# A two-layer attention trunk on one core: layer 0's elementwise work on SBUF goes to POOL, its last gate runs by contraction tiles, the last pair's weights come in six transfers

## The chip, the core and the metric

One core of a Trainium2 chip runs the whole program. Its engines are TensorE (PE, matrix products; loading the weights of one is shown apart, as PEld), VectorE (DVE), ScalarE (ACT), GpSimd (POOL) and SyncE (SP), which here issues all transfers, in order, on one queue. Each engine works through its own instructions in a fixed order and waits at semaphores for the others. PE writes to PSUM; DVE and ACT read PSUM and SBUF; POOL works on SBUF alone here. The metric is the device time of one execution in microseconds.

## What is computed

Two decoder layers over 1024 tokens of width 1024, float32. Each is `h + rmsnorm(mixer(rmsnorm(h)))`. The change is in layer 0, whose mixer is attention in three groups (g = 0, 1, 2) of 16 heads, with dilations 1, 4 and 16; the groups are combined by their softmax denominators, gated and projected:

```
for g, (window, dil) in enumerate(DIL_GROUPS):
    o, lse = dilated_window_attention(q[:, :, sl], k[:, :, sl], v[:, :, sl], window, dil)
alpha = jax.nn.softmax(jnp.stack(lses, axis=0), axis=0)
o = jnp.sum(alpha[..., None] * jnp.stack(outs, axis=0), axis=0)
y = o.reshape(B, S, DIL_WIDTH).astype(h.dtype) * jax.nn.silu(gate)
return y @ w_out
```

Layer 1 is causal differential attention with 8 heads, a norm per head and the same kind of gate.

## The kernel before

**Split operands.** A product needs more precision than one pass gives, so each operand is kept as a high part, rounded to the matmul's type by a copy on ACT, and a low part, the difference, made by `low` (line 122). A projection tile is then three matmuls of 128x512: high by high, low by high, high by low (`project`, line 271). `split` (line 183) makes the two parts of a weight tile, `wh` and `wl`; without a named engine its subtraction alternates between DVE and POOL (`alt`, line 126). The normed input lies in SBUF as XH and XL, by eight contraction tiles kt.

**Order.** PE's order is that of the program text. The order on the other engines is set by a scheduler at build time, from estimates. Tiles come from pools with few buffers, and an instruction that needs a buffer again waits for its last reader.

**Layer 0 up to 400 us** makes the values, seven of the eight gates and their stores. **From 400 us on** it runs a loop over 48 heads (8 pairs of heads, 3 groups, 2 heads), four steps each. A step scores two blocks (`scores`, line 582; DVE adds the mask and takes the maximum, line 603, ACT the exponential), three steps later transposes the probabilities (`transposes`, 611; PE writes `tp`, ACT copies the high part, DVE makes the low part `pp`, line 122), and two steps after that multiplies by the values (`product`, 627). Between these, a filler hands PE the matmuls of the query and key projections to come, one unit per pair and group (`qk_unit`, 220): PE fills two PSUM banks, DVE multiplies them by cos and sin into the tiles t (lines 247 to 251, three buffers), POOL adds and subtracts them into r (250, 252), ACT rounds r to rh (256), and `low` subtracts (DVE and POOL in turn). A unit's parts go to DRAM and come back as the head's qh, ql and ka (`heads_in`, 261).

Group 2 has one block of keys per query block, so its product (`alone`, 654) ends in eight additions per pair: DVE adds the two passes out of PSUM into `us_` (666), ACT copies the upper half to `ul` (667, one buffer), DVE adds both into the group's output tile u (669). Groups 0 and 1 end in `store` (671), whose addition (679) reads PSUM.

**Combination.** When a pair's last scores are done, the statistics go to DRAM (`put_stats`) and come back as js; `joint` (701) forms the weights in eleven small DVE instructions and stores them as wt_d. `combine` (726) loads them spread over 64 partitions as wb (a transfer of 64x512 for each half of the tokens, group and head: 12 a pair, three buffers), multiplies the three u tiles by them (735, DVE and POOL in turn; DVE alone for pair 7), adds them (740), multiplies by the gate sil_in (741) and hands the result to `put_y` (368), which splits it and stores it as y_d. The u tiles have three buffers, so that pair p+1's first u tile is pair p's y.

**End of layer 0.** After the last unit the filler makes the last gate (`late_gates`, `gate_units`, 278): contraction tiles 0 to 3 for both token halves, then 4 to 7. Then `out_early` (420) loads y of the first pairs into XH and XL (`load_y`, 395, each tile as soon as the gate is done with it), multiplies it by the output weights into partial sums, which ACT copies (444) and SP stores in XH and XL (447), and waits for the last heads. `out_rest` closes with the later tiles. Layer 1 has the same tail.

## Time and profile before

| | us |
|---|---|
| median of 3 runs (2026.72 to 2030.63) | 2029.63 |
| the profiled execution | 2031.38 |
| its span in the trace | 2029.5 |
| PE busy in the span | 1905.9 |
| DVE, ACT, POOL busy | 1143.0, 888.0, 618.0 |

The span runs from the first to the last instruction in the trace; the execution is 1.9 us longer. Busy shares are means over stages that differ: layer 0's heads run from 400 to about 1290 us, layer 1's from about 1440 to 1950 us. Matmuls overlap in the trace (a 128x512 one lasts 0.40 us and starts 0.23 us after the one before), so a window in which PE is busy throughout can't be much shortened.

### The profile page before, as it was taken

The numbers are of one execution on the slowest core, as the hardware profiler recorded it, in microseconds if no ns is written. First come the engines' busy times: TensorE is split into PE (matmuls) and PEld (weight loads), VectorE is DVE, ScalarE is ACT, GpSimd is POOL, SyncE is SP. The second block draws the span as 40 slices with busy tenths as digits, with TensorE's granted clock in tenths as the row PEclk, the third lists the DMA queues.
The fourth block names the chain that finished last, engine by engine and source line by source line (L and its number), as shares of the span: only waits on it lengthen the run. The fifth ranks groups of instructions, "written<-read, shape, count | busy, mean of one in ns | idle before, by whom it ended". The sixth has DMA issues, their size and how long they took to land.

```text
span 2029.5 us, 28888 instructions
## 1 busy us (share of the span) xinstructions
PE 1905.9 (94%) x10008; PEld 1594.5 (79%) x10008; DVE 1143.0 (56%) x2771; ACT 888.0 (44%) x2057; POOL 618.0 (30%) x386
## 2 busy tenths in 40 slices
PE   6999999999999998989898978899999999999898
PEld 4788888888878787878787867788878788887776
DVE  3312122146676768676768674571057877878626
ACT  3312122125555555555555565352244445545632
POOL 2000000043353535353535340040471533524111
PEclk8999999999999999999999989999999999999999
DMA  5424244377696969697878889553356555555753
GB/s 208 146 88 140 87 156 152 113 221 229 191 300 195 291 202 293 195 282 218 267 234 240 256 284 294 162 176 107 129 174 193 175 176 164 169 196 182 274 160 125
DMA packets 218018, 397.90 MB, mean 196 GB/s; under 512 B 40976, under 2 KB 123408, under 8 KB 217872
## 3 DMA queue, kind: packets, MB, share of 16 engines
q1 hardware_dynamic: 217872, 396.04, 61.3%
q8 instruction: 80, 1.31, 0.3%
q14 instruction: 66, 0.54, 0.1%
HBM read 254.87 MB, written 132.71 MB: 191 GB/s over the span
## 4 chain that ended last, share of the span: by engine, by line
PE 62%; DMA 13%; DVE 12%; ACT 4%; POOL 4%; issue 3%; SPq 1%; POOLq 0%; DVEq 0%; ACTq 0%
PE pqk L274 22%; PE pv L213 16%; PE pg L274 8%; PE po L386 4%; PE sc L921 2%; PE pe L439 2%; PE up L646 2%; PE sc L596 2%; DMA wb<-wt_d 2%; PE ob L974 2%; DMA st_d<-st 2%; PE tp L619 2%; DVE u L669 1%; POOL r L252 1%; DVE pm L924 1%
## 5 line engine op out<-in xcount | busy, mean ns | idle before, releaser
L274 PE MATMUL pqk<-XL,wh 128*128 128x512 f32 x1024 | 421.1, 411 | 0.0
L274 PE MATMUL pqk<-XH,wh 128*128 128x512 f32 x1024 | 409.3, 400 | 1.7 <-DVE t L251 1.7
L274 PE MATMUL pqk<-XH,wl 128*128 128x512 f32 x1024 | 410.5, 401 | 0.0
L606 ACT ACTIVATE pm<-pm,st 128x128 f32<-128x128 f32 (+1 forms) x384 | 170.2, 444 | 159.7 <-DVE st L603 158.1
L122 POOL TENSOR_TENSOR wl<-raw,wh 128x1024 fp32r<-128x1024 f32 x35 | 84.0, 2400 | 500.6 <-ACT wh L184 500.6
L274 PEld LDWEIGHTS pqk<-XH,wh 128*128 128x128 f32 x1024 | 194.3, 190 | 30.6 <-DVE t L251 2.4
L274 PEld LDWEIGHTS pqk<-XL,wh 128*128 128x128 f32 x1024 | 194.4, 190 | 27.5
L274 PEld LDWEIGHTS pqk<-XH,wl 128*128 128x128 f32 x1024 | 194.8, 190 | 27.0
L250 POOL TENSOR_TENSOR r<-t 128x512 f32<-128x512 f32 x64 | 98.2, 1535 | 266.7 <-DVE t L249 265.7
L122 DVE TENSOR_TENSOR wl<-raw,wh 128x1024 fp32r<-128x1024 f32 x61 | 82.0, 1345 | 149.1 <-ACT wh L184 148.6
L213 PE MATMUL pv<-vwh,XH 128*128 128x512 f32 x384 | 155.8, 406 | 7.0 <-ACT XH L158 4.0
L184 ACT CAST wh<-raw 128x1024 fp32r<-128x1024 f32 x96 | 100.5, 1047 | 140.3 <-PE pqk L274 61.8
L213 PE MATMUL pv<-vwl,XH 128*128 128x512 f32 x384 | 154.9, 403 | 2.8 <-POOL vwl L122 2.8
L213 PE MATMUL pv<-vwh,XL 128*128 128x512 f32 x384 | 154.8, 403 | 0.9 <-DVE XL L122 0.3
L122 DVE TENSOR_TENSOR vs<-pv,vs 128x512 fp32r<-128x512 f32 x64 | 44.2, 691 | 197.3 <-ACT vs L513 191.3
L931 ACT ACTIVATE pm<-pm,mx 128x256 f32<-128x256 f32 (+7 forms) x128 | 99.4, 776 | 120.3 <-DVE mx L930 61.8
L122 DVE TENSOR_TENSOR pp<-tp,pp 128x512 fp32r<-128x512 f32 (+2 forms) x192 | 104.0, 542 | 73.6 <-ACT pp L623 72.0
L619 PE MATMUL tp<-ident,pm 128*128 128x128 f32 x560 | 95.7, 279 | 39.2 <-DVE pp L122 38.2
L603 DVE CUSTOM_DVE_ANT_0 pm<-sc,masks 128x128 f32<-128x128 f32 (+1 forms) x384 | 118.8, 344 | 20.8 <-PE sc L596 19.4
L619 PEld LDWEIGHTS tp<-ident,pm 128*128 128x128 f32 x560 | 72.6, 143 | 73.5 <-issue 34.2
L924 DVE CUSTOM_DVE_ANT_0 pm<-sc,md 128x512 f32<-128x512 f32 (+3 forms) x192 | 102.5, 551 | 32.9 <-PE sc L921 30.1
L513 ACT CAST vs<-pv 128x512 fp32r<-128x512 f32 x48 | 28.2, 587 | 189.9 <-PE pv L213 188.7
(514 smaller groups left out, 4483.6 us busy)
## 6 DMA issues: line engine op xcount, KB each, us to landing
qk_d<-rh SPq DMA_DIRECT2D x64, 512.0 KB
qk_d<-r SPq DMA_DIRECT2D x64, 512.0 KB
qh<-qk_d SPq DMA_DIRECT2D x128, 256.0 KB
ql<-qk_d SPq DMA_DIRECT2D x128, 256.0 KB
ka<-qk_d SPq DMA_DIRECT2D x64, 512.0 KB
v_d<-vs SPq DMA_DIRECT2D x48, 512.0 KB
raw<-in_dil_qk_dram SPq DMA_DIRECT2D x48, 512.0 KB
vt<-v_d SPq DMA_DIRECT2D x48, 512.0 KB
```

The costliest lines, as they stand in the source:

```text
L122: eng.tensor_tensor(o, full, hi.bitcast(F32), ALU.subtract)
L184: nc.scalar.copy(wh, raw)
L213: nc.tensor.matmul(o, lhsT=l, rhs=r_, start=first and k == 0, stop=last and k == 3 * KT - 1, skip_group_check=True)
L250: nc.gpsimd.tensor_sub(put(r[0]), nat(t1), nat(t2))
L274: nc.tensor.matmul(o, lhsT=l[:, kt, :], rhs=r_[:, kt, tok], start=kt == 0 and k == 0, stop=kt == KT - 1 and k == 2)
L386: nc.tensor.matmul(banks[c], lhsT=l[:, kt, ts(n)], rhs=r_[:, ts(c, 512)], start=first and k == 0, stop=last and k == 2,)
L439: nc.tensor.matmul(bank, lhsT=l[:, kt, ts(n)], rhs=r_[:, ts(c, 512)], start=kt == 0 and k == 0, stop=kt == EARLY - 1 and k == 2)
L603: nc.vector.tensor_tensor_reduce(pm[:, cols], sc[:, cols], m[:, m.shape[1] - w_ :], 1.0, 3.0e38, ALU.add, ALU.min, st[:, 0, j : j + 1])
L606: nc.scalar.activation(pm[:, cols], pm[:, cols], AF.Exp, bias=st[:, 0, j : j + 1], scale=-1.0, accum_out=st[:, 1, j : j + 1])
L619: nc.tensor.transpose(out=tp[:, ts(n)], in_=self.pb.pop((b, kb)), identity=ident)
L924: nc.vector.tensor_tensor_reduce(pm[:, k0:k1], sc[:, :w_], m_, 1.0, 3.0e38, ALU.add, ALU.min, mx[:, j : j + 1])
L931: nc.scalar.activation(pm[:, :wq], pm[:, :wq], AF.Exp, bias=mx[:, 0:1], scale=-1.0, accum_out=den)
```

## The change

- `qk_unit`: in layer 0 POOL makes all `wl` and all low parts of r; layer 1 stays as it was.
- `alone`: the last addition (669, now 672) goes from DVE to POOL.
- `combine`: for pairs 0 to 6 POOL does all of it, the two halves of `put_y` included (the rounding copy was ACT's, the difference DVE's). It goes in the order of groups 0, 2, 1, adding as it goes, and the result is built in group 2's tile. The gate tile uses the wb buffers, and u has four buffers. For pair 7 DVE does it as before, with the weights of a head and group in one transfer of 64x1024: six in place of twelve.
- `gate_units`: the last gate of either layer takes tiles 0 and 1 for both halves, then one tile at a time.
- Smaller pools (sr, js, jm, je with one buffer) make room.

```diff
@@ qk_unit
-            split(wh, wl, load(w[half], [P, KT, P]))
+            split(wh, wl, load(w[half], [P, KT, P]), None if on_pool else nc.gpsimd)
...
-            low(nc.vector if on_pool else alt(), r[e].bitcast(F32R), r[e], rh)
+            low(nc.vector if on_pool else nc.gpsimd, r[e].bitcast(F32R), r[e], rh)
@@ gate_units
-                for k0 in (0, EARLY):
+                for kts in ((0, 1), *((kt,) for kt in range(2, KT))):
                     for c in range(2):
-                        yield from project(banks[c], wh, wl, ts(c, 512), range(k0, k0 + EARLY))
+                        yield from project(banks[c], wh, wl, ts(c, 512), kts)
@@ put_y(layer, kt, c, y, hi, eng=None)
-        nc.scalar.copy(hi, y)
-        low(nc.vector, y.bitcast(F32R), y, hi)
+        if eng is None:
+            nc.scalar.copy(hi, y)
+        else:
+            eng.tensor_copy(hi, y)
+        low(eng or nc.vector, y.bitcast(F32R), y, hi)
@@ alone
-                nc.vector.tensor_add(by_residue(uo, SUB[2])[:, 2 * c : 2 * c + 2, :], us_[:HD], ul)
+                nc.gpsimd.tensor_add(by_residue(uo, SUB[2])[:, 2 * c : 2 * c + 2, :], us_[:HD], ul)
@@ combine
+            eng = nc.vector if pr == 7 else nc.gpsimd
+            full = {}
+            if pr == 7:
+                for g, tag in ((0, "v"), (2, "v"), (1, "pp")):
+                    full[g] = lp.tile([P, T], F32R, tag=tag, name="wb").bitcast(F32)
+                    for h in range(2):
+                        nc.sync.dma_start(full[g][64 * h : 64 * h + 64], wt_d[2 * pr + h, g].partition_broadcast(64))
             for c in range(2):
                 tok = ts(c, 512)
-                for g in range(NG):
-                    wb = lp.tile([P, 512], F32, tag="wb", name="wb", bufs=3)
...
-                    (nc.vector if pr == 7 else alt()).tensor_mul(us[g][:, tok], us[g][:, tok], wb)
-                sil = lp.tile([P, 512], F32, tag="sil_in", name="sil_in", bufs=1)
+                y = us[2][:, tok]
+                for g in (0, 2, 1):
+                    if full:
+                        wb = full[g][:, tok]
+                    else:
+                        wb = lp.tile([P, 512], F32, tag="wb", name="wb", bufs=3)
...
+                    eng.tensor_mul(us[g][:, tok], us[g][:, tok], wb)
+                    if g:
+                        eng.tensor_add(y, y, us[1 if g == 1 else 0][:, tok])
+                sil = lp.tile([P, 512], F32, tag="wb", name="sil_in", bufs=3)
                 nc.sync.dma_start(sil, sil_d[0][pr, :, tok])
-                y = us[0][:, tok]
-                for g in (1, 2):
-                    (nc.vector if pr == 7 else nc.gpsimd).tensor_add(y, y, us[g][:, tok])
-                nc.vector.tensor_mul(y, y, sil)
-                put_y(0, pr, c, y, us[1][:, tok])
+                eng.tensor_mul(y, y, sil)
+                put_y(0, pr, c, y, us[1][:, tok], eng)
@@ the loop over heads
-                    us[hd.pr, hd.g] = lp.tile([P, T], F32, tag="u", name="u", bufs=3)
+                    us[hd.pr, hd.g] = lp.tile([P, T], F32, tag="u", name="u", bufs=4)
```

In the whole program DVE issues 24 `wl`, 24 low parts of r, 64 additions of `alone`, 21 weight multiplications, 14 gate multiplications and 14 low parts of y fewer, ACT 14 copies fewer, and POOL these and no others more; PE issues the same matmuls in the same number. The lines of the changed kernel are shifted (603 is 606, 666 is 669, 669 is 672, 679 is 682, 735 is 750, 740 is 752, 741 is 755).

Where the order of the engines changes, in three places. First DVE in pair 0's combination, from the sixth addition of `alone` on. Before:

```order
L666 TENSOR_TENSOR us__3776<-us__3776,up_3773 128x256
L669 TENSOR_TENSOR u_3270<-us__3776,ul_3777 64x2x128
L735 TENSOR_TENSOR u_2602<-u_2602,wb_3900 128x512
L122 TENSOR_TENSOR pp_3806<-tp_3801,pp_3806 128x512
L666 TENSOR_TENSOR us__3816<-us__3816,up_3813 128x256
L603 ISA pm_3827,st_3652<-sc_3826,masks_2246 128x128
L603 ISA st_3652 128x1
L603 ISA pm_3827,st_3652<-sc_3826,masks_2246 128x256
L603 ISA st_3652 128x1
L669 TENSOR_TENSOR u_3270<-us__3816,ul_3817 64x2x128
L249 TENSOR_TENSOR t_3863<-pqk_3783,sin_2236 128x512
L122 TENSOR_TENSOR wl_4293<-raw_4294,wh_4292 128x1024
```

and now:

```order
L669 TENSOR_TENSOR us__3776<-us__3776,up_3773 128x256
L122 TENSOR_TENSOR pp_3806<-tp_3801,pp_3806 128x512
L669 TENSOR_TENSOR us__3816<-us__3816,up_3813 128x256
L606 ISA pm_3827,st_3652<-sc_3826,masks_2246 128x128
L606 ISA st_3652 128x1
L606 ISA pm_3827,st_3652<-sc_3826,masks_2246 128x256
L606 ISA st_3652 128x1
L249 TENSOR_TENSOR t_3863<-pqk_3783,sin_2236 128x512
```

Gone from between the low parts `pp` and the maxima are the weight multiplication, both additions into u and the `wl`; a little further down so are two more multiplications and a low part of r.

Second, POOL in the same place, from the `wl` before the first weight multiplication to the first r of the next unit. Before:

```order
L122 TENSOR_TENSOR wl_3889<-raw_3890,wh_3888 128x1024
L735 TENSOR_TENSOR u_2907<-u_2907,wb_3904 128x512
L740 TENSOR_TENSOR u_2602<-u_2602,u_2907 128x512
L735 TENSOR_TENSOR u_2602<-u_2602,wb_3921 128x512
L250 TENSOR_TENSOR r_3500<-t_3862,t_3863 128x64x8
L252 TENSOR_TENSOR r_3501<-t_3865,t_3864 128x64x8
L740 TENSOR_TENSOR u_2602<-u_2602,u_2907 128x512
L735 TENSOR_TENSOR u_3270<-u_3270,wb_3929 128x512
L122 TENSOR_TENSOR r_3501<-r_3501,rh_3877 128x1024
L740 TENSOR_TENSOR u_2602<-u_2602,u_3270 128x512 x2
L250 TENSOR_TENSOR r_3894<-t_4098,t_4099 128x512
```

and now, up to the same unit's second r:

```order
L122 TENSOR_TENSOR wl_3889<-raw_3890,wh_3888 128x1024
L672 TENSOR_TENSOR u_3270<-us__3776,ul_3777 64x2x128
L750 TENSOR_TENSOR u_2602<-u_2602,wb_3900 128x512
L672 TENSOR_TENSOR u_3270<-us__3816,ul_3817 64x2x128
L750 TENSOR_TENSOR u_2907<-u_2907,wb_3909 128x512
L122 TENSOR_TENSOR wl_4293<-raw_4294,wh_4292 128x1024
L250 TENSOR_TENSOR r_3500<-t_3862,t_3863 128x64x8
L672 TENSOR_TENSOR u_3270<-us__3855,ul_3856 64x2x128
L750 TENSOR_TENSOR u_2602<-u_2602,wb_3921 128x512
L750 TENSOR_TENSOR u_3270<-u_3270,wb_3904 128x512
L252 TENSOR_TENSOR r_3501<-t_3865,t_3864 128x64x8
```

(u_2602, u_2907 and u_3270 are pair 0's groups 0, 1 and 2.) After it stand a low part of r, an addition, a low part of r, two multiplications and two additions, and then the next unit's r_3894. Between the first weight multiplication and r_3500 there are now three instructions where there were two, with a `wl` of 1024 columns among them, and three between r_3500 and r_3501 where there was none.

Third, SP at the last pair's weights. Before:

```order
L733 DMA wb_11756<-wt_d_62 64x512 x2
L733 DMA wb_11760<-wt_d_62 64x512 x2
L733 DMA wb_11764<-wt_d_62 64x512 x2
L737 DMA sil_in_11768<-sil_d0_65 128x512
L447 DMA XH_78<-part_11713 128x4x128
```

and now:

```order
L738 DMA wb_11737<-wt_d_62 64x1024
L738 DMA wb_11743<-wt_d_62 64x1024
L738 DMA wb_11737<-wt_d_62 64x1024
L738 DMA wb_11740<-wt_d_62 64x1024 x2
L738 DMA wb_11743<-wt_d_62 64x1024
L450 DMA XH_78<-part_11713 128x4x128
```

The six transfers stand directly before the store of the partial sum; both gate tiles of pair 7 are now loaded some 25 rows earlier.

## Rows read from the trace of the kernel before

**Rows 1.** The page's first part, whole execution: for each engine its busy time in us (share of the span) and its number of instructions.

```profile
PE 1905.9 (94%) x10008; PEld 1594.5 (79%) x10008; DVE 1143.0 (56%) x2771; ACT 888.0 (44%) x2057; POOL 618.0 (30%) x386
```

**Rows 2.** Busy time by windows of 50 us. Columns: window, its length, then for PE, PEld, DVE, ACT and POOL the busy us with the number of instructions, then TensorE's granted clock (1.00 is the level of 2.4 GHz), the DMA engines' busy share and GB/s.

```profile
500.00:550.00 50.00, 50.00 (x280) 42.55 (x278) 33.88 (x102) 26.05 (x80) 16.31 (x10) 1.00 0.72 208
550.00:600.00 50.00, 44.11 (x244) 37.04 (x243) 39.16 (x90) 27.70 (x72) 26.74 (x16) 0.97 0.89 265
...
650.00:700.00 50.00, 43.94 (x241) 36.69 (x240) 38.62 (x94) 27.67 (x73) 25.96 (x15) 0.97 0.80 239
...
750.00:800.00 50.00, 43.82 (x248) 36.30 (x247) 39.46 (x100) 27.01 (x73) 25.34 (x15) 1.00 0.78 237
...
850.00:900.00 50.00, 43.38 (x235) 35.86 (x235) 38.33 (x91) 25.03 (x67) 25.12 (x15) 0.97 0.74 230
...
950.00:1000.00 50.00, 43.83 (x230) 36.57 (x229) 39.52 (x99) 26.34 (x76) 24.37 (x15) 0.93 0.78 234
...
1050.00:1100.00 50.00, 42.60 (x237) 35.39 (x236) 41.14 (x96) 25.60 (x76) 23.60 (x15) 1.00 0.78 241
...
1150.00:1200.00 50.00, 44.41 (x233) 36.94 (x231) 38.82 (x98) 27.62 (x79) 23.86 (x15) 0.93 0.81 256
1200.00:1250.00 50.00, 36.93 (x185) 29.80 (x183) 20.82 (x63) 27.87 (x70) 3.99 (x2) 0.83 1.04 345
1250.00:1300.00 50.00, 44.74 (x213) 36.37 (x212) 30.58 (x75) 24.62 (x65) 4.82 (x2) 0.93 0.66 195
```

**Rows 3.** Who waited for whom on PE, whole execution, the longest entry: us in total, times, the longest one.

```profile
PE tp L619 <- DVE pp L122: 38.2, 19, 3.4
```

**Rows 4.** Timeline of DVE in the first combination (pair 0): start, us, what, and in brackets the engine's idle time before it and what ended that.

```profile
554.67 0.69 DVE L735 TENSOR_TENSOR u<-u,wb 128x512 f32<-128x512 f32 x1 [2.18 <-DMA wb<-wt_d]
...
558.72 1.26 DVE L122 TENSOR_TENSOR wl<-raw,wh 128x1024 fp32r<-128x1024 f32 x1
...
560.58 0.68 DVE L122 TENSOR_TENSOR pp<-tp,pp 128x512 fp32r<-128x512 f32 x1
...
562.40 0.69 DVE L251 TENSOR_TENSOR t<-pqk,cos 128x512 f32<-128x512 f32 x1 [0.81 <-POOL r L250]
...
563.61 2.32 DVE L122 TENSOR_TENSOR r<-r,rh 128x1024 fp32r<-128x1024 f32 x1
565.96 1.56 DVE L669 TENSOR_TENSOR u<-us__3855,ul 64x256 f32<-64x256 f32 x1
...
568.24 0.69 DVE L122 TENSOR_TENSOR pp<-tp,pp 128x512 fp32r<-128x512 f32 x1
568.85 2.91 DVE L735 TENSOR_TENSOR u<-u,wb 128x512 f32<-128x512 f32 x1
```

**Rows 5.** Timeline of POOL in the same stretch.

```profile
556.07 1.29 POOL L735 TENSOR_TENSOR u<-u,wb 128x512 f32<-128x512 f32 x1 [5.13 <-DVE pp L122]
...
558.85 2.26 POOL L735 TENSOR_TENSOR u<-u,wb 128x512 f32<-128x512 f32 x1
561.08 1.29 POOL L250 TENSOR_TENSOR r<-t 128x512 f32<-128x512 f32 x1
563.17 1.68 POOL L252 TENSOR_TENSOR r<-t 128x512 f32<-128x512 f32 x1 [0.80 <-DVE t L251]
...
568.83 2.38 POOL L122 TENSOR_TENSOR r<-r,rh 128x1024 fp32r<-128x1024 f32 x1
...
579.10 1.29 POOL L250 TENSOR_TENSOR r<-t 128x512 f32<-128x512 f32 x1 [4.96 <-DVE t L249]
```

**Rows 6.** Groups of instructions on POOL, equal shapes together: count | busy us, mean ns of one | idle time of the engine just before them, and what ended most of it.

```profile
L122 POOL TENSOR_TENSOR wl<-raw,wh 128x1024 fp32r<-128x1024 f32 x35 | 84.0, 2400 | 500.6 <-ACT wh L184 500.6
...
L122 POOL TENSOR_TENSOR r<-r,rh 128x1024 fp32r<-128x1024 f32 x24 | 58.5, 2437 | 19.7 <-ACT rh L256 19.7
...
L735 POOL TENSOR_TENSOR u<-u,wb 128x512 f32<-128x512 f32 x21 | 31.5, 1501 | 41.5 <-DMA wb<-wt_d 26.1 <-DVE t L249 6.9 <-DVE pp L122 5.1
```

**Rows 7.** The same for DVE, and under it, for line 669 alone between 400 and 1300 us, DVE's busy time with the number of instructions, the granted clock, the DMA share and GB/s.

```profile
L122 DVE TENSOR_TENSOR wl<-raw,wh 128x1024 fp32r<-128x1024 f32 x61 | 82.0, 1345 | 149.1 <-ACT wh L184 148.6
...
L122 DVE TENSOR_TENSOR r<-r,rh 128x1024 fp32r<-128x1024 f32 x40 | 58.9, 1473 | 20.0 <-ACT rh L256 20.0
...
L735 DVE TENSOR_TENSOR u<-u,wb 128x512 f32<-128x512 f32 x27 | 32.2, 1196 | 18.2 <-DMA wb<-wt_d 18.2
...
400.00:1300.00 900.00, 63.24 (x64) 0.97 0.79 242
```

**Rows 8.** One operand's instructions, the small joint softmax on DVE: count, and shortest/median/longest in ns.

```profile
L714 DVE TENSOR_TENSOR je<-jm,js x24: 159/164/1297, 543.8 to 1269.4; 128x16 f32<-128x16 f32 x24
```

**Rows 9.** Timeline of the DMA issues on SP's queue: the weights of pair 0, a head's load after pair 6, and the last pair's weights with the store of a partial sum behind them.

```profile
550.42 7.41 SPq L733 DMA_DIRECT2D wb<-wt_d  x9
...
1192.93 1.57 SPq L266 DMA_DIRECT2D qh<-qk_d  x2
...
1274.06 8.96 SPq L733 DMA_DIRECT2D wb<-wt_d  x12
...
1284.89 0.66 SPq L447 DMA_DIRECT2D XH<-part  x1
```

**Rows 10.** Who waited for whom on PE between 1176 and 1300 us.

```profile
PE sc L596 <- DMA ka<-qk_d: 6.0, 1, 6.0
PE pe L439 <- ACT part L444: 5.2, 1, 5.2
```

More of the change, by code (lines that the diff above doesn't have):

```diff
@@ L366, in trunk, with put_y @@
     stored = set()
-    def put_y(layer, kt, c, y, hi):
+    def put_y(layer, kt, c, y, hi, eng=None):
         tok = ts(c, 512)
@@ L685, in put_stats @@
                 nc.tensor.transpose(out=tp[:32, :P], in_=st.rearrange("p h e b -> p (h e b)"), identity=ident)
-                sr = lp.tile([32, P], F32, tag="sr", name="sr")
+                sr = lp.tile([32, P], F32, tag="sr", name="sr", bufs=1)
                 nc.vector.tensor_copy(sr, tp[:32, :P])
@@ L701, in joint @@
         def joint(pr):
-            s = lp.tile([P, NG, 2, 16], F32, tag="js", name="js")
+            s = lp.tile([P, NG, 2, 16], F32, tag="js", name="js", bufs=1)
             for h in range(2):
@@ L708, in joint @@
             m, den = s[:, :, 0, :], s[:, :, 1, :]
-            mx = lp.tile([P, 16], F32, tag="jm", name="jm")
-            e = lp.tile([P, NG, 16], F32, tag="je", name="je")
+            mx = lp.tile([P, 16], F32, tag="jm", name="jm", bufs=1)
+            e = lp.tile([P, NG, 16], F32, tag="je", name="je", bufs=1)
             nc.vector.tensor_tensor(mx, m[:, 0, :], m[:, 1, :], ALU.min)
@@ L727, in combine @@
             fill.until(("gate", 0, pr))
+            eng = nc.vector if pr == 7 else nc.gpsimd
[5 more added lines that the diff above has]
+                        nc.sync.dma_start(full[g][64 * h : 64 * h + 64], wt_d[2 * pr + h, g].partition_broadcast(64))
             for c in range(2):
                 tok = ts(c, 512)
[L730 to L742 removed]
+                y = us[2][:, tok]
[4 more added lines that the diff above has]
+                        wb = lp.tile([P, 512], F32, tag="wb", name="wb", bufs=3)
+                        for h in range(2):
+                            nc.sync.dma_start(
+                                wb[64 * h : 64 * h + 64], wt_d[2 * pr + h, g, tok].partition_broadcast(64))
+                    eng.tensor_mul(us[g][:, tok], us[g][:, tok], wb)
+                    if g:
+                        eng.tensor_add(y, y, us[1 if g == 1 else 0][:, tok])
+                sil = lp.tile([P, 512], F32, tag="wb", name="sil_in", bufs=3)
+                nc.sync.dma_start(sil, sil_d[0][pr, :, tok])
+                eng.tensor_mul(y, y, sil)
+                put_y(0, pr, c, y, us[1][:, tok], eng)
         units = [(pr, g) for pr in range(8) for g in range(NG)]
```

3 lines of the change are left out of this document (removed).

## The prediction

> **What bounds the kernel now.** I read the windows first. From 500 us on, one window of 50 us is full of PE work (50.00 of 50.00 between 500 and 550) and the next is not [rows 2]. With matmuls back to back nothing but PE matters in the full windows, so the time to be had lies in the others. They recur every 104 us, once a pair, where a pair is combined. For pairs 0 to 5 PE's idle time there is 5.89 + 6.06 + 6.18 + 6.62 + 6.17 + 7.40 = 38.3 us, and a granted clock below 1.00 in four of them costs another (0.03 + 0.03 + 0.03 + 0.07) x 50 = 8.0 us: 46.3 us, 7.7 a pair. The list of waits names one releaser for nearly all of it: PE's transposes wait for the low part `pp` on DVE, 38.2 us in 19 times [rows 3], that is three a pair. A second such region is the end of layer 0: from 1150 to 1300 us PE idles 5.59 + 13.07 + 5.26 = 23.9 us, and the clock costs (0.07 + 0.17 + 0.07) x 50 = 15.5, together 39.4 us.
>
> Then I asked why DVE is late with `pp`, although it is busy only 56% of the span [rows 1]. Pair 0's timeline [rows 4] shows three reasons in a row. It sat 2.18 us before a weight multiplication whose wb had not landed. It sat 0.81 us until POOL's r released a buffer of t. And its instructions on SBUF were long where POOL was at work: a low part of r of 2.32 us, an addition of 1.56, a weight multiplication of 2.91, where the `wl` of the same shape took 1.26, the mean addition 63.24 / 64 = 0.99 [rows 7] and the multiplication at 554.67 just 0.69. The last began at 568.85, just after POOL's low part of r at 568.83, which ran to 571.21 [rows 5]: 2.3 us of waiting and its own time. It goes the other way too: POOL's multiplication at 558.85 took 2.26, with DVE's `wl` at 558.72 ahead of it. But the low part at 560.58, which reads PSUM, took its 0.68 in the midst of that same POOL instruction. So DVE and POOL shut each other out on two-input work in SBUF, and an input in PSUM escapes it.
>
> The Trainium skill (SBUF — State Buffer, "SBUF: two separate sides") says that the shared port pair is an exclusive lock, held for a whole instruction, which a DVE instruction needs that has two SBUF inputs. The trace agrees, with the 2.91 us. By it the eleven instructions of `joint`, which stay on DVE, would still lose up to one POOL instruction each.
>
> **The change, part by part.**
>
> *Off DVE*: 24 `wl` x 1.345 = 32.3, 24 low parts of r x 1.473 = 35.4, 64 additions = 63.2, 21 multiplications x 1.196 = 25.1 [rows 7], and 28 gate multiplications and differences at the 0.69 of the multiplication in rows 4, 19.3: 175 us, all but the three pieces of `pp`, maxima and rope that PE waits for. What was bought with it is not the busy time but the place: none of these stands ahead of a `pp` any more.
>
> *Onto POOL*: 48 instructions of 1024 columns x 2.40 = 115 [rows 6], 49 of 512 columns x 1.29 [rows 5] = 63, 64 additions of 256 columns and 14 roundings. The trace has no POOL instruction of either kind. From 1.29 for 512 and 2.40 for 1024 columns the slope is 2.17 ns a column, so I take 0.74 us for an addition (an estimate; 64 of them 47 us). For a one-input rounding the bounds are 0.74 and 1.29, 10 to 18 us; I take the lower, since it reads half as much. POOL goes from 618 to about 855 us, less what it no longer waits for DVE. A pair costs it 12 r x 1.29 + 12 x 2.40 + 8 x 0.74 + 14 x 1.29 + 2 x 0.74 = 70 us of the 96 that PE needs for a pair: enough on the whole, but not in the combination.
>
> *The combination on POOL, walked through for pair 0*. The wb of the first multiplication lands when it did, some 4.5 us after its issue at 550.4 [rows 9], say 555.3 (one issue later, by the order of SP). From there the r of the running unit comes after 1.29 + 0.74 + 1.29 + 2.40 and ends at 562.3; it ended at 562.37 before [rows 5]. The second ends after 0.74 + 3 x 1.29 more at 566.9 (before: 564.85). The first r of the next unit ends after two low parts of r and six instructions of 1.29 more, at 579.5 (before: 580.39). So POOL does not get earlier, and PE, freed of its waits, arrives 6 to 7 us sooner. What covers it: `pp` and the maxima up to that point are no longer behind DVE's waits; the t tile that DVE waits for holds a PSUM bank which PE needs again only after 24 further projection matmuls (24 x 0.23 us and what stands between, some 10 us); transposes and scores have two banks each, a step of 4 us apart. DVE would wait some 4 to 6 us at the second place, and one or two steps of cover are 4 to 8. I take 2 us of PE idle a pair as what is left, between 0 and 4: a gain of 5.7 x 6 = 34 us, from 46 down to 22.
>
> *ACT* loses 14 roundings, but its copy to `ul` now waits for POOL's addition of the step before (one buffer). Behind it on ACT are the exponentials and the high part of `pp`. In the walk that addition ends at 557.3, before the copy is due; its price is in the 2 us. *The fourth u buffer* takes away a wait for y's store; the trace shows none of weight there, so nothing.
>
> *End of layer 0.* Pair 6's combination is like the others, 5.7 us; but the next head's loads were issued at 1192.93 [rows 9] behind y and wb transfers, which don't get faster, so half of it is given back: 3 us. From 1200 to 1250 us the transfers run at 345 GB/s and the DMA engines are full [rows 2]; PE waits there for a head's ka (6.0 us [rows 10]). The bytes stay the same. The gate by contractions frees XH and XL two tiles earlier, and on SP their loads then stand ahead of that head's: 0, between -6 and +8. In the last pair twelve issues took 8.96 us [rows 9]; six take half, and the store of the partial sum at 1284.89, for which ACT and then PE waited 5.2 us [rows 10], comes 4.5 us earlier, the gate tile's load no longer being ahead of it. DVE does this pair as before, and its y is needed only after some 54 matmuls of 0.23 us. Bounds 2 and 5.2. Together 3 + 0 + 4.5 = 7.5 us, from -3 to +18.
>
> *Layer 1* keeps its engines and its order but for the last gate; there two loads come ahead of a head's: 0, between -3 and +3.
>
> The sum: 34 + 7.5 = 41.5 us off the profiled execution's 2031.4 (span 2029.5), which stands 0.1% above the median: **1990 us**. The bounds together give 2031.4 - 67 to 2031.4 - 16, or 1964 to 2015, and 1962 with the median's 2 us.
>
> **The rivals.**
>
> *POOL takes the place of DVE.* In the walk the r's are as late as before; if PE's cover is shorter than I think, DVE waits for t where it waited for wb, with `pp` behind it. For it: POOL has some 40 us of unbroken work after wb lands. Against: DVE's own share of the delay is gone. Price: 6 us a pair stay, 6 x 1.7 = 10 us are gained, and 4.5 at the last pair: 2017, from 2010 to 2026. The Trainium skill (GPSIMD Engine Reference, "Engine selection") advises VectorE for elementwise work, since GpSimd takes about twice as long for two inputs. The trace agrees on the duration (2.40 against 1.26 us); by that rule this rival would win.
>
> *Slower: SP held up by POOL.* The wb buffers now serve the gate tile too, and SP issues in order. A pair's last three loads wait until POOL is done with the first ones, which now takes until about 575 us in the walk, and the next head's qh, ql and ka stand behind. It decides if such a load is issued later than the 4 steps, 16 us, ahead of its use that it has. Then PE waits for ka as it did once at the end (6.0 us), beside what is left now: 12 us a pair, 4.3 more than today, over seven pairs +30: 2060. Against it: before, the gate tile with a single buffer held SP in the same way.
>
> *No change*: the gain per pair and new waits of POOL's lock against `joint` (three instructions of `joint` reached 1.30 us at the longest against 0.16 [rows 8]; eleven at 1.1 each are 12 us of DVE, of which a third may show on PE): 2031.
>
> **How the numbers follow.** Forecast 0.60 (1962 to 2010), POOL as the bound 0.20 (2010 to 2026), slower 0.13, no change 0.07. A measurement here can tell about 0.2%, 4 us, from none. Faster by more: 0.60 and nearly all of the second, 0.18, 0.78; within: 0.07 and the rest of the second, 0.09; slower 0.13. The range takes the first two cases: 1962 to 2026.
>
> **What would show it.** Right: the windows of pairs 0 to 5 with over 48 us of PE and a clock of 1.00; the wait of PE for `pp` at a third of 38.2 us; no DVE instruction on PSUM longer than now; POOL near 850 us, DVE near 970; no wait for ACT's partial sum at the end. Wrong: PE's transposes waiting as long as now, with DVE waiting for r or ACT for POOL's addition; SP standing at wb or the gate tile with heads' loads behind; POOL's addition of 256 columns well over 0.74 us.

## The result, and the profile after

The changed kernel takes 2001.66 us (median of 4 runs, 1993.94 to 2009.15) against 2030.13 us (4 runs): a ratio of 0.985, 95% interval 0.982 to 0.989. The forecast was 1990 us, between 1962 and 2026. The profiled execution is the longest of the four: 2009.15 us, span 2007.4. In a second set of runs, below, the ratio is 0.983.

The page's first part after, to be held against [rows 1]:

```profile
PE 1898.1 (95%) x10008; PEld 1593.7 (79%) x10008; DVE 975.2 (49%) x2610; ACT 884.9 (44%) x2043; POOL 797.1 (40%) x561
```

DVE lost 167.8 us (175 were forecast) and POOL gained 179.1 (237). The POOL groups show what made most of the difference: columns as in [rows 6], the kernel before in the first line.

```profile
L252 POOL TENSOR_TENSOR r<-t 128x512 f32<-128x512 f32 x48 | 79.4, 1654 | 80.6 <-DVE t L251 46.2 <-DVE jm L712 32.1 <-DMA ql<-qk_d 2.3
```

```profile
L252 POOL TENSOR_TENSOR r<-t 128x512 f32<-128x512 f32 x48 | 62.3, 1297 | 22.8 <-DVE t L251 19.3 <-DVE jm L715 2.8
L750 POOL TENSOR_TENSOR u<-u,wb 128x512 f32<-128x512 f32 x42 | 53.8, 1294 | 39.0 <-DMA wb<-wt_d 25.2 <-ACT pm L609 13.6
...
L379 POOL CAST u<-u 128x512 fp32r<-128x512 f32 x14 | 8.6, 611 | 0.1
```

POOL's r takes 1297 ns on average where it took 1654, the multiplication by wb 1294 where it took 1501 [rows 6], and the rounding of one input 0.61 us, where 0.74 to 1.29 was bounded. Most of DVE's two-input work in SBUF, beside which POOL's instructions were long, is gone from layer 0.

The windows, columns as in [rows 2], pairs 0 to 5 and then the end of layer 0:

```profile
550.00:600.00 50.00, 49.01 (x283) 41.85 (x282) 25.92 (x80) 28.84 (x75) 43.00 (x31) 1.00 0.97 300
650.00:700.00 50.00, 47.33 (x261) 39.66 (x260) 24.33 (x73) 26.44 (x70) 41.91 (x31) 0.97 0.97 292
750.00:800.00 50.00, 47.96 (x268) 40.80 (x268) 24.99 (x76) 26.43 (x69) 41.97 (x30) 0.97 0.96 292
850.00:900.00 50.00, 47.62 (x265) 40.50 (x265) 25.11 (x78) 26.17 (x70) 42.48 (x30) 0.97 0.96 293
950.00:1000.00 50.00, 47.82 (x268) 40.71 (x266) 24.63 (x76) 26.42 (x71) 41.99 (x29) 0.97 0.98 292
1050.00:1100.00 50.00, 47.43 (x256) 40.10 (x255) 23.44 (x70) 25.02 (x65) 40.34 (x29) 0.93 0.94 282
1150.00:1200.00 50.00, 29.45 (x156) 25.02 (x155) 17.84 (x48) 24.89 (x57) 30.97 (x23) 0.76 1.04 327
1200.00:1250.00 50.00, 42.75 (x238) 36.44 (x237) 21.87 (x82) 30.10 (x88) 8.45 (x7) 0.90 0.89 260
```

By the prediction's way of counting, pairs 0 to 5 now cost 0.99 + 2.67 + 2.04 + 2.38 + 2.18 + 2.57 = 12.8 us of PE idle time and (4 x 0.03 + 0.07) x 50 = 9.5 us by the clock, 22.3 in place of 46.3 [rows 2]. (What the clock costs is an estimate, from the mean granted clock of a window.) The end of layer 0 is no better than it was: in the window from 1150 PE is busy for 29.45 us, with the DMA engines full and the clock at 0.76.

PE's longest waits in layers 0 and 1 (us in total, times, the longest); other entries are left out:

```profile
PE pe L442 <- DMA XH<-y_d: 13.0, 1, 13.0
PE pqk L274 <- DVE t L251: 12.4, 6, 2.4
...
PE pg L274 <- DVE t L251: 7.6, 1, 7.6
PE sc L599 <- DMA ka<-qk_d: 7.3, 1, 7.3
PE sc L935 <- DMA ka<-qk_d: 6.8, 2, 5.8
```

The wait for `pp`, 38.2 us [rows 3], is gone. In its place stands one of 2.4 us at the most for DVE's t, six times, and three long ones at the end of layer 0: for a y tile in XH, for t at the last gate, for ka.

Three stages can be told apart by PE's timeline, by the first matmul of the last gate (`pg`) and the first transposition of layer 1's input (`pt_x`); the second set's profiled execution is beside them:

| us | before | after | again |
|---|---|---|---|
| first `pg` starts | 1176.1 | 1148.6 | 1137.4 |
| from there to the first `pt_x` | 146.6 | 150.5 | 150.1 |
| from there to the span's end | 706.8 | 708.3 | 711.0 |

The gain is all in the pairs, 27.5 us and 38.7 us (the second against the same profile of before, from another set of runs). The end of layer 0 takes 4 us more, and what follows 1.5 to 4 us more. The last figure is no larger than the spread: that stage takes 706.6 to 713.5 us in nine profiles with the new gate order (these two and seven of the experiments), and 704.8 to 711.3 in three with the old one.

How a pair waits now, POOL first, in pair 1's combination (start, us, what, idle time before it and what ended that):

```profile
655.35 1.30 POOL L250 TENSOR_TENSOR r<-t 128x512 f32<-128x512 f32 x1
...
660.66 2.52 POOL L750 TENSOR_TENSOR u<-u,wb 128x512 f32<-128x512 f32 x2 [3.19 <-DMA wb<-wt_d]
663.14 1.31 POOL L252 TENSOR_TENSOR r<-t 128x512 f32<-128x512 f32 x1
```

and DVE in the same stretch:

```profile
664.48 0.69 DVE L248 TENSOR_TENSOR t<-pqk,sin 128x512 f32<-128x512 f32 x1 [3.25 <-POOL r L252]
...
676.65 0.69 DVE L251 TENSOR_TENSOR t<-pqk,cos 128x512 f32<-128x512 f32 x1 [3.22 <-POOL r L250]
```

The multiplications by wb at 660.66 waited 3.19 us for their weights; r (line 252) stands behind them in POOL's queue and DVE's t behind r, since it needs the buffer that r reads. It is the wait of the kernel before, one engine further back. Between 500 and 1140 us DVE now stands 72.4 us at t for POOL's r, up to 4.8 at a time, where it was 4.1 us before. Some `pp` stand behind such a wait, but they still come in time: PE never waits for them, and feels the late t alone, with up to 2.4 us.

### The profile page after: what moved, and what is told of

The parts are those of the page before. It is cut to its first block, busy times and chain, and to the rows that moved or that the text cites. A ratio compares the mean times of both kernels' runs of the same rounds, so it can differ in the third digit from the quotient of the medians.

```text
span 2007.4 us, 29105 instructions
## 1 busy us (share of the span) xinstructions
PE 1898.1 (95%) x10008; PEld 1593.7 (79%) x10008; DVE 975.2 (49%) x2610; ACT 884.9 (44%) x2043; POOL 797.1 (40%) x561
## 4 chain that ended last, share of the span: by engine, by line
PE 62%; DMA 14%; DVE 8%; POOL 7%; issue 4%; ACT 3%; SPq 2%; POOLq 0%; ACTq 0%; DVEq 0%
PE pqk L274 22%; PE pv L213 16%; PE pg L274 8%; DMA wb<-wt_d 4%; PE po L389 4%; PE sc L599 2%; PE sc L935 2%; POOL u L750 2%; DMA ka<-qk_d 2%; PE up L649 2%; PE pe L442 2%; PE ob L988 1%; PE tp L622 1%; DVE pm L938 1%; DMA st_d<-st 1%
## 5 line engine op out<-in xcount | busy, mean ns | idle before, releaser
L274 PE MATMUL pqk<-XH,wh 128*128 128x512 f32 x1024 | 411.4, 402 | 12.4 <-DVE t L251 12.4
L122 POOL TENSOR_TENSOR wl<-raw,wh 128x1024 fp32r<-128x1024 f32 x59 | 141.6, 2401 | 511.1 <-ACT wh L184 509.8
L626 ACT CAST pp<-tp 128x512 fp32r<-128x512 f32 (+2 forms) x192 | 89.4, 466 | 81.5 <-PE up L649 61.3
L122 POOL TENSOR_TENSOR r<-r,rh 128x1024 fp32r<-128x1024 f32 x48 | 115.2, 2401 | 24.4 <-ACT rh L256 24.4
L250 POOL TENSOR_TENSOR r<-t 128x512 f32<-128x512 f32 x64 | 84.4, 1318 | 91.4 <-DVE t L249 90.4
L122 DVE TENSOR_TENSOR wl<-raw,wh 128x1024 fp32r<-128x1024 f32 x37 | 50.9, 1376 | 138.1 <-ACT wh L184 137.8
```

The costliest lines, as they stand in the source:

```text
L122: eng.tensor_tensor(o, full, hi.bitcast(F32), ALU.subtract)
L250: nc.gpsimd.tensor_sub(put(r[0]), nat(t1), nat(t2))
L274: nc.tensor.matmul(o, lhsT=l[:, kt, :], rhs=r_[:, kt, tok], start=kt == 0 and k == 0, stop=kt == KT - 1 and k == 2)
L626: nc.scalar.copy(pp[:, 0, :w_], tp[:, :w_])
```

## The experiments

Twelve runs in three batches of four, each timed beside the kernel before on the same chip. Ratios are to that kernel.

| run | the changed kernel, but | ratio | 95% interval |
|---|---|---|---|
| again | nothing | 0.983 | 0.981 to 0.985 |
| u3 | three u buffers | 0.997 | 0.996 to 0.999 |
| u3t4 | three u, four t buffers | 0.996 | 0.995 to 0.997 |
| combine_back | combination on both engines | 0.994 | 0.992 to 0.996 |
| splits_back | splits on both engines | 0.996 | 0.994 to 0.998 |
| alone_back | additions of `alone` on DVE | 0.985 | 0.983 to 0.987 |
| only_u4 | all of these three back | 0.995 | 0.993 to 0.997 |
| twelve | last pair's weights in twelve transfers | 0.983 | 0.981 to 0.985 |
| gate_halves, halves_2 | last gates in halves | 0.981, 0.981 | 0.979 to 0.982, 0.978 to 0.984 |
| dve6 | pair 6's combination on DVE | 0.983 | 0.981 to 0.986 |
| jam_less | 4.6 MB of loads left out | 0.975 | 0.973 to 0.978 |

**again**: the changed kernel itself.

> The changed kernel itself, once more, as the ruler for the other three. The four runs so far lie between 1993.9 and 2009.2 us, far wider than before's, and its ratio to before is 0.985. If the spread belongs to the kernel, these runs spread as much and the ratio falls between 0.982 and 0.989; if the first four were odd, the runs now agree within 0.3%.

The four runs lie between 1997.0 and 2000.3 us, within 0.2% of each other, so the spread of the first four did not come again here; the ratio fits both cases. (In later sets the kernels spread by up to 0.8%.) The windows of its profile, two of the six pairs and the sum over the six, and its wait for t:

```profile
650.00:700.00 50.00, 47.89 (x276) 40.91 (x275) 25.71 (x79) 27.62 (x74) 43.59 (x31) 1.00 0.97 296
...
1050.00:1100.00 50.00, 48.21 (x277) 41.10 (x276) 25.57 (x79) 26.14 (x73) 39.22 (x27) 1.00 0.93 297
sum 300.00, PE 289.52 PEld 246.60 DVE 157.86 ACT 161.80 POOL 247.69; mean PE 48.25 PEld 41.10 DVE 26.31 ACT 26.97 POOL 41.28
```

```profile
PE pqk L274 <- DVE t L251: 10.0, 7, 2.2
```

The waits are nearly those of the first profile (10.0 and 12.4 us; PE idle 300 - 289.52 = 10.5 and 12.8 us), but the granted clock is 1.00 in all six windows. So 9.5 us of the first profile's count in the pairs are the clock, which two executions of the same program were granted differently. That accounts for most of the 11.2 us by which the pairs of the two profiles differ. What decided it was not tried; that the two ran on the same chip is not on record.

**u3**: the fourth u buffer undone.

```diff
-us[hd.pr, hd.g] = lp.tile([P, T], F32, tag="u", name="u", bufs=4)
+us[hd.pr, hd.g] = lp.tile([P, T], F32, tag="u", name="u", bufs=3)
```

> The changed kernel with three u buffers as before. The prediction put the fourth at nothing: then the time is that of the changed kernel within 0.2%. Rival: since POOL finishes pair p's y some 10 us later than DVE did, the next pair's first sums now wait for the stores of y, ACT's copy and DVE's addition with them, and the kernel is 1 to 3 us a pair slower, 7 to 20 us.

The rival's direction was right, and its price too small: nearly all of the gain is gone. In pair 0's combination:

```profile
576.20 0.68 DVE L682 TENSOR_TENSOR u<-up,ul 64x512 f32<-64x512 f32 x1 [4.51 <-POOL u L752]
576.92 0.58 ACT L677 COPY ul<-up 64x512 f32<-64x512 f32 x1 [4.56 <-DVE u L682]
...
576.99 1.19 PE L649 MATMUL up<-pp,vt 128*128 128x256 f32 x4 [5.92 <-issue]
```

DVE's addition into the next pair's u waits 4.51 us for the last reader of the old one. That is POOL's addition at line 752, and not a store of y, which the prediction and the rival had named. ACT's next copy waits for DVE, and PE, which the profile shows waiting for nothing, starts 0.1 us after the addition has read its bank of `up` (576.20 + 0.68 = 576.88). That PE waited for this bank is read from these times, since the profile names no releaser. PE stands so once a pair, 31.6 us in six times.

**u3t4**: with that, a fourth t buffer in the room that u left.

```diff
-tag="t", name="t", bufs=3 - on_pool)
+tag="t", name="t", bufs=4 - 2 * on_pool)
```

> Three u buffers and, in their room, a fourth t buffer. Against the run with three u buffers alone: if PE's waits for DVE's t (12.4 us in six times between 500 and 1150 us) come from DVE standing at a t buffer that POOL's r still reads, a fourth buffer lets DVE go on and frees PE's bank: these waits fall below 4 us in all, the granted clock stays at 1.00, and it is 10 to 20 us faster. Rival: POOL is late by more than one step, DVE stands at the next buffer instead, and the gain is under 4 us.

Inconclusive for t: with three u buffers the waits for t were down to 0.5 us already, and the wait for `up` stayed (26.7 us in six times). Against three u buffers alone the time is 2.5 us less, inside the intervals. Four of both were not run.

**combine_back** and **splits_back**: one half of the move undone in each.

```diff
-                    eng.tensor_mul(us[g][:, tok], us[g][:, tok], wb)
+                    (nc.vector if pr == 7 else alt()).tensor_mul(us[g][:, tok], us[g][:, tok], wb)
...
-                eng.tensor_mul(y, y, sil)
-                put_y(0, pr, c, y, us[1][:, tok], eng)
+                nc.vector.tensor_mul(y, y, sil)
+                put_y(0, pr, c, y, us[1][:, tok], None)
```

> The changed kernel with the combination's work shared again: the weight multiplications of pairs 0 to 6 on DVE and POOL in turn, the gate multiplication and the low part of y on DVE, the rounding on ACT; splits and the additions of alone stay on POOL. Theory A, that the combination on DVE stood ahead of the low parts pp: PE's wait for pp comes back with 1.5 to 3 us a pair, and the kernel is 10 to 20 us slower than the changed one. Theory B, that the splits and additions were what delayed pp, and that POOL is now what PE waits for: POOL is relieved of 3 multiplications, the gate's and the rounding, r comes earlier, the waits for t fall, and the kernel is up to 10 us faster.

```diff
-            split(wh, wl, load(w[half], [P, KT, P]), None if on_pool else nc.gpsimd)
+            split(wh, wl, load(w[half], [P, KT, P]))
...
-            low(nc.vector if on_pool else nc.gpsimd, r[e].bitcast(F32R), r[e], rh)
+            low(nc.vector if on_pool else alt(), r[e].bitcast(F32R), r[e], rh)
```

> The changed kernel with the splits of layer 0 (wl and the low parts of r) on DVE and POOL in turn, as before; the combination stays on POOL. Theory A, that it is the place in DVE's queue that counts: three or four of these instructions stand in each combination, up to 2.4 us each while POOL works, so PE's wait for pp comes back with 1 to 2 us a pair and the kernel is 6 to 12 us slower than the changed one. Theory B, that POOL's queue is the bound of the changed kernel: POOL loses about three instructions of 2.40 us in each combination, r comes up to 5 us earlier, PE's waits for t (2.1 us a pair) and the clock that falls with them go, and the kernel is 10 to 20 us faster.

The time is theory A's in both, beyond its upper end: medians of 2021.6 and 2024.0 us against 1998.0 on the same chip. PE's longest wait between 500 and 1140 us, first with the combination shared, then with the splits shared:

```profile
PE tps L688 <- DVE pp L122: 19.8, 6, 3.8
```

```profile
PE tp L622 <- DVE pp L122: 21.0, 12, 3.0
```

In each, the wait for `pp` is back at 20 us, and the wait for t is down to 0.2 and 3.6 us. But it comes back by different ways. With the combination shared, the steps that stand on DVE ahead of the `pp` are the combination's own, as theory A had it; in pair 0:

```profile
575.77 1.74 DVE L755 TENSOR_TENSOR u<-u,sil_in 128x512 f32<-128x512 f32 x1 [1.85 <-POOL u L752]
...
578.19 1.00 DVE L122 TENSOR_TENSOR u<-u 128x512 fp32r<-128x512 f32 x1
579.11 0.68 DVE L122 TENSOR_TENSOR pp<-tp,pp 128x512 fp32r<-128x512 f32 x1
```

With the splits shared no split stands there. In each pair the longest wait (2.8 to 3.0 us, 17 of the 21) follows two waits of DVE, for POOL's r and for ACT's copy:

```profile
567.07 0.69 DVE L248 TENSOR_TENSOR t<-pqk,sin 128x512 f32<-128x512 f32 x1 [3.53 <-POOL r L252]
569.26 0.68 DVE L682 TENSOR_TENSOR u<-up,ul 64x512 f32<-64x512 f32 x1 [1.50 <-ACT ul L677]
```

and DVE's splits, at 1.25 and 1.22 us on average, were not held up. The scheduler had put this addition (682) and the `pp` behind it after the t of line 248; in the changed kernel both come before it (in pair 1 the `pp` starts at 660.69, and t at 664.48). So undoing this edit also changed DVE's order, and the run doesn't tell the splits' own worth from the order's.

**alone_back**: line 672 on DVE again.

```diff
-                nc.gpsimd.tensor_add(by_residue(uo, SUB[2])[:, 2 * c : 2 * c + 2, :], us_[:HD], ul)
+                nc.vector.tensor_add(by_residue(uo, SUB[2])[:, 2 * c : 2 * c + 2, :], us_[:HD], ul)
```

> The changed kernel with the last additions of alone on DVE as before (64 of 256 columns, 0.65 to 1.56 us there, 0.74 on POOL). If POOL's queue is the bound in the combination, three additions less in it bring r forward by 2 us and the kernel is up to 8 us faster; if what stands on DVE ahead of pp decides, PE's wait for pp comes back with 0.5 to 1 us a pair and it is 3 to 6 us slower.

A wait for `pp` of 6.6 us in six times came back, as the second case had it, and the wait for t stayed at again's size (10.1 and 10.0 us). The ratio is 0.2% above again's, inside the intervals: not settled. (Before, these additions took 0.60 to 2.74 us, not 0.65 to 1.56.)

**only_u4**: the edits of the last three together, and the gates in halves.

> Of the change only the fourth u buffer, the smaller pools and the last pair's six transfers stay: splits, combination, the additions of alone and the gates' halves are as before (the combination keeps the new order of groups). Theory A, that the parts complete each other (u tiles, DVE's combination and DVE's splits each make PE wait as long as one of them is left): PE waits for pp as it did before, some 35 us between 500 and 1150 us, and the time is within 0.3% of before, ratio 0.997 to 1.003. Theory B, that the fourth u buffer is the gain by itself, since taking it away cost 1.4%: ratio 0.985 to 0.990.

Neither number: a ratio of 0.995, nearer to A. Between 500 and 1140 us PE waits for `pp` as often as before, but less long each time (before it was 36.4 us in 18 times, of the 38.2 of [rows 3]):

```profile
PE tp L622 <- DVE pp L122: 26.7, 18, 2.6
```

So what is left of the change (the buffer, the new order of groups, the gate tile in the wb buffers, the smaller pools, the six transfers) brings about 0.5%, a third of the gain; it was not told apart, but that the transfers bring nothing is seen in twelve, below. The rest needs the combination and the splits on POOL, and the fourth buffer: each of the three, taken away alone, costs 1.1 to 1.4%, together more than twice the gain. With only the combination on POOL, or only the splits, each with the additions of `alone`, the time is that of neither (0.996 and 0.994, against 0.995).

**gate_halves**, and **halves_2** on another chip: the last gates' order undone.

```diff
-                for kts in ((0, 1), *((kt,) for kt in range(2, KT))):
+                for kts in (range(0, EARLY), range(EARLY, KT)):
```

> The changed kernel with the last gates in two halves of contraction tiles as before. Theory A: the new order asks for the gate's second PSUM bank after 6 matmuls in place of 12, so PE's wait of 7.6 us for DVE's t at that bank falls to 3 to 4 us, and the kernel is 4 us faster. Theory B: what sets the end of layer 0 is the load of y's later tiles, which SP issues at 1184.65 us, behind the weights that wait for POOL in the combination of pair 6; then the wait for t falls as well, but the wait for XH (13.0 us) grows by the same, and the time stays within 2 us. By the prediction's own term (tiles free two earlier, worth 0) also within 2 us, with neither wait changed.

> The kernel with the gates in halves once more, on the chip of these three. The first time its ratio to before was 0.981 against 0.983 for the changed kernel on the same chip, with intervals that overlap, and the end of layer 0 took the same time in both. If the halves are no gain, the ratio now lies at 0.983 or above.

For layer 0 neither theory, but the third case, the prediction's own term: the wait for t at the gate is 6.4 and 7.9 us (7.6 with the change), and y makes PE wait 13.0 and 11.9 us (13.0). Only the wait for ka, 7.3 us with the change, is gone, and waits of about 3 us for vt stand in its place; from the first `pg` to the first `pt_x` it takes 151.6 and 148.7 us, against 150.5 and 150.1. Both ratios lie 0.2% under again's, below the 0.983 that was to show no gain; with intervals that overlap this is a hint, not established, that the new order costs some 4 us. Between 1800 and 1975 us, at layer 1's last gate, PE waits for a head's ka 5.8 and 6.3 us with the change (after, again), and in halves_2

```profile
PE sc L935 <- DMA ka<-qk_d: 2.5, 1, 2.5
```

(in gate_halves 4.6 us, for XH). Whether this is the difference is not shown: behind `pt_x` halves_2 takes 704.8 us, but gate_halves 711.3, as long as again.

**jam_less**: fewer bytes at the end of layer 0. It leaves out layer 0's loads of the low parts of y and both norm tables, so that its product and its norms work on what stood in the tiles.

```diff
-        for e, x in enumerate((XH, XL)):
+        for e, x in enumerate((XH, XL)[: 1 + layer]):
...
-            nc.sync.dma_start(cos, a["norm_post"][0].partition_broadcast(P))
-            nc.sync.dma_start(sin, a["norm_pre"][1].partition_broadcast(P))
```

> The changed kernel with seven loads of layer 0's low parts of y (512 KB each) and the two loads of the norm tables (512 KB each) left out, 4.6 MB less between 1160 and 1230 us; layer 0's product and norms then work on what stood in these tiles. SP still issues XH's third tile behind four weight loads of pair 6. Theory A, full DMA engines set the end of layer 0: PE's wait for XH (13.0 us) falls under 4 us and the wait for ka (7.0 us) under 3, 10 to 16 us less in all. Theory B, SP's place behind the weights that wait for POOL sets it: XH's third tile is issued as long after the gate's wait as now, some 25 us after it ended, a wait of 7 us or more stays, and it is 4 to 7 us faster.

Theory A by its waits (XH's not quite under 4 us), but with less time behind them. PE's waits at the end of layer 0:

```profile
PE pg L274 <- DVE t L251: 7.3, 1, 7.3
PE pe L442 <- DMA XH<-y_d: 4.3, 1, 4.3
...
PE sc L599 <- DMA ka<-qk_d: 2.0, 1, 2.0
```

(7.5, 13.0 and 7.0 us in again.) From the first `pg` to the first `pt_x` it takes 141.9 us, against 150.1 in again and 149.7 in dve6: 8 us less, where 10 to 16 were expected. The median of 1982.4 us is 16 us under the 1998.1 of dve6 on the same chip, but the rest of that lies behind `pt_x`, where jam_less takes 700.1 us and again and dve6 711.0 and 710.0; why layer 1, which then works on other numbers, is shorter was not tried. SP's timeline in the changed kernel, at the end of layer 0 and at the last pair:

```profile
1170.91 4.15 SPq L748 DMA_DIRECT2D wb<-wt_d  x4
...
1184.23 0.38 SPq L754 DMA_DIRECT2D sil_in<-sil_d  x1
1184.65 1.62 SPq L400 DMA_DIRECT2D XH<-y_d  x2
...
1251.96 3.69 SPq L738 DMA_DIRECT2D wb<-wt_d  x6
1255.75 0.65 SPq L450 DMA_DIRECT2D XH<-part  x1
```

XH's third tile is issued at 1184.65, behind four weight loads and the gate tile that wait for POOL, which waits for weights; that is 26.0 us after PE's wait at the gate ended (1158.62). In jam_less, with the same order there, it is 17.5 us (1147.65 and 1165.10). This fits full engines that act through SP's place: weights that land sooner let SP go on. It is not fully told apart, since jam_less also has nine issues fewer on SP's queue.

**dve6**: pair 6 like pair 7.

```diff
-            eng = nc.vector if pr == 7 else nc.gpsimd
+            eng = nc.vector if pr >= 6 else nc.gpsimd
```

> The changed kernel with pair 6's combination on DVE, as pair 7's is. If POOL's multiplication, which waits for its weights ahead of the last r, is what makes PE wait 7.5 us for t at the gate's second bank, that wait falls under 4 us; the weights' buffers come free sooner (0.69 us a multiplication in place of 1.29), SP gets to y's loads sooner, the wait for XH falls by 3 to 6 us, and the kernel is 4 to 10 us faster. If it is the full DMA engines, the waits only change places and the time stays within 3 us; DVE waiting for the weights ahead of pp adds up to 3 us.

The second case. In the changed kernel the wait at the gate's bank is a chain over three engines:

```profile
1155.34 1.26 POOL L750 TENSOR_TENSOR u<-u,wb 128x512 f32<-128x512 f32 x1 [2.28 <-DMA wb<-wt_d]
1156.56 1.28 POOL L250 TENSOR_TENSOR r<-t 128x512 f32<-128x512 f32 x1
...
1157.87 0.69 DVE L251 TENSOR_TENSOR t<-pqk,cos 128x512 f32<-128x512 f32 x1 [3.78 <-POOL r L250]
...
1158.62 0.80 PE L274 MATMUL pg<-XH,wh 128*128 128x512 f32 x1 [7.57 <-DVE t L251]
```

With the multiplications on DVE the wait at the bank is still 6.5 us, since DVE now stands before them:

```profile
1138.41 0.69 DVE L750 TENSOR_TENSOR u<-u,wb 128x512 f32<-128x512 f32 x1 [3.58 <-DMA wb<-wt_d]
...
1150.57 0.76 DVE L750 TENSOR_TENSOR u<-u,wb 128x512 f32<-128x512 f32 x1 [3.48 <-DMA wb<-wt_d]
```

y makes PE wait 9.8 us and ka 3.1, less by 3 and 4 than in again. PE waits longer in other places, 2.7 us more for ACT's partial sums and 1.0 for a `pp`, and the stage from `pg` to `pt_x` takes 149.7 us (150.1). Whichever engine multiplies waits for the weights, and t is behind.

**twelve**: the transfers halved again.

```diff
-                        nc.sync.dma_start(full[g][64 * h : 64 * h + 64], wt_d[2 * pr + h, g].partition_broadcast(64))
+                        for c in range(2):
+                            nc.sync.dma_start(full[g][64 * h : 64 * h + 64, ts(c, 512)], wt_d[2 * pr + h, g, ts(c, 512)].partition_broadcast(64))
```

> The changed kernel with the last pair's weights in twelve transfers of 64x512 in place of six of 64x1024. By the prediction's term for the six transfers it loses about 4.5 us: the store of the partial sum is issued behind twelve issues, and PE waits about 5 us longer for ACT. Rival: the partial sum's buffers wait for the landing of the stores, which the DMA engines set and not SP's issues, and the time stays within 2 us.

The rival. SP's timeline and ACT's copy that waits for the store, and then the same copy in the changed kernel (its SP rows are above):

```profile
1239.20 8.11 SPq L739 DMA_DIRECT2D wb<-wt_d  x12
1247.41 0.65 SPq L450 DMA_DIRECT2D XH<-part  x1
```

```profile
1250.60 0.58 ACT L447 COPY part<-pe 128x512 f32<-128x512 f32 x1 [7.01 <-DMA XH<-part]
```

```profile
1263.49 0.58 ACT L447 COPY part<-pe 128x512 f32<-128x512 f32 x1 [6.35 <-DMA XH<-part]
```

With twelve transfers the issues take 8.11 us, with six 3.69; from the first issue to the copy it is 1250.60 - 1239.20 = 11.4 us with twelve and 1263.49 - 1251.96 = 11.5 with six. So the number of issues doesn't set it, and the bytes are the same. The copy in the kernel before:

```profile
1288.11 0.59 ACT L444 COPY part<-pe 128x512 f32<-128x512 f32 x1 [3.01 <-DMA XH<-part]
```

From its first issue (1274.06 [rows 9]) that is 14.1 us: the store does land 2.5 us sooner now, but as much so with twelve. What brought it was not tried; of the differences there, the gate tile's load no longer stands between the weights and the store. PE's wait at that place is 2.0 us, and 2.7 with twelve, where it was 5.2 [rows 10]. Six transfers bring the last pair's y later, too: ACT gets it 15.5 us after the first issue (1251.96 to 1267.43), and 12.3 with twelve (1239.20 to 1251.50). The times (0.983 both) show no cost of that.

## Why the prediction was right, and where it was not

*DVE's queue ahead of `pp`.* Right in the main: the wait for `pp` went from 38.2 us to nothing. For the combination the experiment shows the way as well, since its steps stood ahead of `pp` again when it was shared. For the splits only the trace of before speaks (the low part of r of 2.32 us in [rows 4]); the run that shared them brought the wait back by another order on DVE. The Trainium skill (SBUF — State Buffer, "SBUF: two separate sides") tells of a lock between DVE and POOL. The trace agrees: POOL's r (line 252) went from 1654 to 1297 ns on average when DVE's two-input work left. The eleven instructions of `joint` lost little: 22.4 us in all before and 19.9 now, though line 720's eight take 615 ns on average, where the same instruction took 167. That is 2.5 us a pair, where the rival of no change had 12.

*POOL's walk.* Right in its ends, with some luck: the three r's of pair 0 were forecast to end at 562.3, 566.9 and 579.5, and ended at 558.8, 565.7 and 577.9. POOL's first multiplication began at 551.7 and not at 555.3, since the weights were stored 3 us earlier; and POOL then waited 2.25 us for the next wb, which the walk didn't have. The two errors offset each other in part. PE's idle time left was put at 2 us a pair, between 0 and 4, and is 12.8 / 6 = 2.1. The term of 34 us (22 to 46) measured 46.3 - 22.3 = 24.0 in the first profile and 46.3 - 10.5 = 35.8 in the second; 9.5 us of the difference are the clock. That POOL takes DVE's place, the first rival, is what the waits show, at 2 us a pair and not at 6.

*The signs.* POOL's addition took 0.73 to 0.76 us, once 1.59, and DVE's 975 us were forecast as 970. PE over 48 us in a pair's window with a clock of 1.00 holds in one of six windows of the first profile, and on average in the second (48.25). That PE would no longer wait for ACT's partial sum was wrong: it waits 2.0 and 3.1 us.

*The fourth u buffer at nothing.* Wrong as a price of that edit, though not in the sum. It was read from the kernel before, where y was done early; with POOL's later combination, the buffer is worth 1.4%. The step that failed is looking for an edit's cover in the trace of before, when another edit of the same change moves what covers it. That the buffer was in the change all the same is luck for the forecast: without it the gain is 0.3%.

*End of layer 0, 7.5 us faster.* Wrong in sign: 4 us slower, just outside its bound of 3. Two of its terms failed. The store of the partial sum was to come 4.5 us earlier by six transfers: it comes 2.5 us earlier, with six as with twelve, and PE waits for ACT a second time there, 3.1 us. And half of pair 6's gain was to stay: the gate's wait is 7.6 us (3.0 before), since POOL's multiplication waits for wb ahead of the last r, and y's wait is 13.0 (4.2 before). The row that spoke against both stood among those read: DMA engines at 1.04, 345 GB/s [rows 2].

*Layer 1 at nothing, between -3 and +3.* 1.5 and 4.2 us slower, which the spread of that stage covers.

*The slower rival, SP held up by POOL.* Not in pairs 0 to 5, where PE hardly waits for a load (0.3 us). At the end of layer 0 it happens, with the DMA engines as the likely cause: jam_less eased it, though it left out issues as well as bytes.

The 41.5 us forecast were 34 + 7.5 + 0. Measured were 27.5 - 3.9 - 1.5 = 22.1 us between the two profiled executions, and 38.7 - 3.5 - 4.2 = 31.0 in the second. The total lies within the range because the pairs, by far the largest term, came out near their forecast.

## What to carry to other kernels

Where one engine's queue holds both what the bound engine waits for and work that waits for a transfer or for another engine, look at moving the second kind off as a whole: here the combination without the splits, or the splits without the combination, brought no more than neither. Price an edit's cover in the kernel as changed, not in the trace of before: a buffer worth nothing there can carry the whole gain. Where a scheduler sets the order, undoing one edit tests the edit and a new order together: look in the trace which of them brought the wait back. And read a gain by stages before calling it one stage's: half of what jam_less gained lay outside the stage that was meant. Where the DMA engines are full, fewer issues only moved the wait here, and fewer bytes shortened it.

## What was not expected of the hardware

ACT's copy, which waits for a store issued behind the weights, began 11.4 us after the first issue with twelve transfers of 64x512 and 11.5 with six of 64x1024, the same 1.5 MB written. Two executions of the same program with like waits were granted clocks of 0.97 and 1.00 in the same windows, worth 9.5 us in the count above. In pair 1 of the first, PE waited 2.34 us for t (until 677.40), and from 679.20 to 682.40 matmuls of 128x512 that follow each other start 0.43 us apart, at the 1.2 GHz level; in again, after a wait of 2.11 us (until 677.09), they keep to 0.23.
